# A planned feed-forward stage takes over the computed end times of the stage before it, and the last norm joins the plan

## The chip, the cores and the metric

The kernel runs on one core of one Trainium2 chip, in one launch. The metric is device time in microseconds from the first to the last instruction with what lies around it; lower is better. TensorE is called PE here, VectorE DVE, ScalarE ACT, GpSimd POOL; SP is the engine that issues most of the loads and stores.

## The reference

One layer of a hybrid decoder: two half-step SwiGLU feed-forward parts around a token mixer, and a norm over each row at the end. All values are fp32; 256 tokens, a width of 2048, a feed-forward width of 5632.

```python
def rms_norm(x, gain):
    var = mean(x * x, axis=-1); return x * rsqrt(var + 1e-6) * gain

def swiglu_ffn(x, w_gate, w_up, w_down):
    return (silu(x @ w_gate) * (x @ w_up)) @ w_down

x = x + 0.5 * swiglu_ffn(rms_norm(x, ffn1_norm), ffn1_w_gate, ffn1_w_up, ffn1_w_down)
x = x + mixer(rms_norm(x, mix_norm))          # gated recurrence and short convolution
x = x + 0.5 * swiglu_ffn(rms_norm(x, ffn2_norm), ffn2_w_gate, ffn2_w_up, ffn2_w_down)
return rms_norm(x, final_norm)
```

## The kernel before

**Tiling.** The 256 tokens are two row tiles, `t` = 0 and 1, of 128 each. `xres` holds the running sum; a chunk `c` is 512 of its 2048 columns. Hidden columns are treated in units of 512.

**Products.** An fp32 weight block is loaded into a `raw` tile and split into a high part (a rounding copy, `CAST` on ACT) and a low part (raw minus high, on DVE); PE multiplies high by the high and low parts of the other operand, and low by the high part. Blocks of two by two are multiplied with seven products instead of eight where sums allow it: a block ("sevens") has the units p0, p2, p3, p4, p5, p6, p1, whose weights or activations are sums of blocks, and x01, x00, x11, x10, which are plain. The weight sums are made by adding raw tiles, on DVE or by an accumulating DMA that POOL issues. Each unit adds into one of four PSUM banks, a, c, d and e; copies of a bank (`u_`, `s_`, or bank to bank) are taken on ACT between units. In a down stage `hv` is a sum of activations of two hidden units and `hs` its high and low part, the operand of p4, p5, p6 and p2.

**Stages.** Each feed-forward part (`tag` 1 and 2) begins with hand-ordered pieces (`first_blocks`, `fifth`, `down`). Then follow, for `s` = 1 and 3, a `fine_stage` (two gate blocks and two up blocks) and a `down_stage` (two blocks) that adds its result to `xres`. The results of an up block are multiplied with the gates (`gated_by`, the tile `z`), turned by PE (`ph`), and split into the high and low parts of the hidden activations `h`.

**What sets the order.** Each of these stages is laid out by a `Plan`. A step has an engine, an estimated length, the steps it needs, an earliest time `at`, and perhaps a `due` time. PE's order, unit by unit, is written in the tables `down_orders` and `fine_orders` ("j" or "-" ahead says whether bank c starts from bank e, "T" is where activations are turned, "n0" and "n1" are pieces of the next stage's norm). For the other engines the plan takes, among the steps that could start soonest, the one with the earliest latest time. The instructions are then issued in that order, and each engine works its own queue in order: an instruction that waits holds all behind it on its engine.

**From stage to stage.** A plan's clock is zero at the estimated end of PE's work in the plan before. `settled` hands over the times at which engines and buffers come free. Three kinds of steps belong to results of the stage before but are issued in the next one: the residual updates (`handed`), the last two gating products (`tails`), and the splits of the last turned activations (`later`). In the kernel before these enter with fixed times:

```python
for fn in handed:
    plan.add("DVE", add_ps, fn, at=0.1, due=12.0)
...
for key, high, low in later:
    turned[key] = turned_parts(plan, high, low, at=-2.0)
for (fn, cell), at in zip(tails, (-3.3, 0.1)):
    cell["step"] = plan.add("DVE", add_ps, fn, at=at, due=2.0)
```

**The end.** In the last down stage of the second part, `last` squares each finished chunk on ACT and multiplies it with the gain on DVE. The last chunk of row t=0 comes out of PE in two halves of 256 columns (`ps_d_last`). After the plan, `finish` issues by hand, in program order: `close` for row t=1 (square, root, the factor `fr` by one refined step, scaling of the row in four pieces and four stores), then for each half of row t=0 the update of `xres`, its square and its product `y`, and after the second half the factor, the scaling and the stores.

Of the kernel before, what the change touches and what calls it, by code (L numbers as in the profile page):

```python
# [176 lines left out]
def hybrid_block(ctx: ExitStack, tc: tile.TileContext, a: dict, out: bass.AP):  # L177
# [40 lines left out]
    def bank(name):  # L218
        return psum.tile([P, 512], F32, tag="ps", name=name)
# [522 lines left out]
    def ffn(tag, norm, after, opening=False):  # L742
        with tc.tile_pool(name=f"ffn{tag}", bufs=1, side="left", reuse_waits="tile") as fp:
# [298 lines left out]
            def down():  # L1042
# [60 lines left out]
                return updates  # L1103
# [169 lines left out]
            def turn_item(plan, u, t, h, *needs, later=None):  # L1273
# [20 lines left out]
                if later is not None:  # L1294
                    later.append(((u, t), high, low))
                    return None
                return turned_parts(plan, high, low, a)

            def sevens(plan, w, cs, name, sf, rows, xs, rooms, order, pairs, result, fills=None, down=False, joint=False, final=None):
# [107 lines left out]
                for key in order:  # L1407
# [24 lines left out]
                    if final is not None and key == units_only[-1]:  # L1432

                        def halves(u=u, q=q):
                            hi, lo = u.tiles["hi"], u.tiles["lo"]
                            for o in (slice(0, CW // 2), slice(CW // 2, CW)):
                                final.append(bank(f"ps_{name}_last")[:, : CW // 2])
                                parts = [(hi[:, j, o], lo[:, j, o]) for j in range(UK)]
                                multiply([(final[-1], sf[q], True, True)], parts)

                        u.low = plan.add("PE", 24 * 0.12, halves, *u.hi, *u.lo, *(fills or {}).get(q, []))
                        u.high.append(u.low)
                        continue
# [43 lines left out]
            def up_result(plan, sg, later):  # L1487
                def result(t, n, ps, done, keys, snaps, made):
# [28 lines left out]
            def pinned(plan):  # L1517
# [7 lines left out]
                    ["-", "p0", "p4", "x01", "p2", "p5", "x11", "p6", "p1", "p3", "x10", "x00"],  # L1525
                ),
                (
                    ["j", "p0", "p4", "T", "x01", "x11", "p5", "p1", "p6", "x00", "p2", "x10", "p3"],
                    ["-", "p0", "p4", "n1", "p2", "p1", "n0", "p5", "x11", "p6", "x00", "x10", "x01", "p3"],
# [3 lines left out]
                    ["-", "p0", "p4", "x01", "p2", "p5", "x11", "p6", "x00", "p3", "x10", "p1"],  # L1533
# [24 lines left out]
            def fine_stage(s, free, ready, handed):  # L1558
                plan = Plan(free, ready)
                for fn in handed:  # L1560
                    plan.add("DVE", add_ps, fn, at=0.1, due=12.0)
# [26 lines left out]
                return plan, tails, later  # L1588

            def down_stage(s, free, ready, tails, later, final=None):  # L1590
                plan = Plan(free, ready)
                turned, cells = {}, []
                for key, high, low in later:
                    turned[key] = turned_parts(plan, high, low, at=-2.0)
                for (fn, cell), at in zip(tails, (-3.3, 0.1)):
# [77 lines left out]
                return plan, handed  # L1673
# [13 lines left out]
            for s in (1, 3):  # L1687
# [435 lines left out]
    def last(plan, c, t, z):  # L2123
        if "fin" not in held:
            held["fin"] = bigs.tile([P, D], F32, tag="big", name="fin")
            nc.scalar.dma_start(held["fin"], a["final_norm"].partition_broadcast(P))
            held["roots"] = []
        fin = held["fin"]
        if c == NC_D - 1:
            return  # L2130
# [15 lines left out]
        def gain():  # L2146
            lastgain = fin[:, D - CW :]
            dve.tensor_scalar(lastgain, lastgain, -0.5, None, op0=ALU.mult)

        squared = plan.add("ACT", 0.65, square, z, due=10.0)  # L2150
        plan.add("DVE", 0.65, lambda: dve.scalar_tensor_tensor(xr, xr, -0.5, fin[:, cs], op0=ALU.mult, op1=ALU.mult), squared, due=25.0)
        held.setdefault(("squared", t), []).append(squared)
        if len(held["squared", t]) == NC_D - 1:
            pre = plan.add("DVE", 0.4, before, *held["squared", t], due=4.0)
            plan.add("ACT", 0.3, lambda: act.activation(single("root"), held[t], AF.Sqrt), pre, due=4.0)
            if t == 0:
                plan.add("DVE", 0.35, gain, pre, due=4.0)

    def finish(keep, halves):
        y = [keep(f"y_{t}") for t in range(NT)]  # L2160
        Engine.pinned = True
        close(1, y[1], 0, 1)
        w = CW // 2
        for h in range(2):
            xh = xres[:, 0, D - CW + h * w : D - CW + (h + 1) * w]
            dve.scalar_tensor_tensor(xh, halves[h], 0.5, xh, op0=ALU.mult, op1=ALU.add)
            close(0, y[0], h, 2)

    def close(t, y3, h, n):

        fin, w = held["fin"], CW // n

        def single(tag):
            return work.tile([P, 1], F32, tag=tag, name=f"{tag}_{t}_{h}")

        o = slice(D - CW + h * w, D - CW + (h + 1) * w)
        part = single("part")
        junk = work.tile([P, CW], F32, tag="junk", name=f"junk_f_{t}_{h}", bufs=1)
        act.activation(junk[:, :w], xres[:, t, o], AF.Square, accum_out=part)
        dve.tensor_tensor(y3[:, h * w : (h + 1) * w], xres[:, t, o], fin[:, o], op=ALU.mult)  # L2180
        if h < n - 1:
            held["part"] = part
            return
# [50 lines left out]
```

## Time and profile before

| what | value |
|---|---|
| time, median of 3 runs | 1715.39 us (1714.71 to 1715.41) |
| profiled run, its own time | 1715.2 us |
| span of that execution | 1713.4 us |
| granted clock of TensorE | 0.999 |
| TensorE busy | 1700.1 us, 99% |
| VectorE busy | 1547.2 us, 90% |
| ScalarE busy | 1110.6 us, 65% |
| GpSimd busy | 56.0 us, 3% |
| HBM read | 339.82 MB |

Times within the profile are from the start of the span. A busy time is that of one engine; a row of the timeline gives start, length, engine, operation, result and operands, and in square brackets how long the engine had been idle and what released it. In the program's names a number of the buffer is left out, so that `lo_d_p` is the low part of the weights of any p unit of a down block, and `raw_d_w` any raw tile of them.

### The profile page before, as it was taken

To read this page: it belongs to the slowest core of one execution; us is meant where nothing else is said; L and a number is where in the kernel's file an instruction comes from. 1 tells how busy PE (TensorE), PEld (TensorE's weight loads), DVE (VectorE), ACT (ScalarE), POOL (GpSimd) and SP (SyncE) were. 2 spreads that over 40 slices of the span, in tenths; PEclk is the share of its full clock that TensorE was granted. 3 is DMA by queue.
4 is the path that set the end of the run, shared out by engine and by line. 5 is a ranking of instruction groups with operands and counts; after the bars stand their busy time and mean duration, and the time that the engine had idled before them with its cause. 6 is when DMAs were issued, how large, how long until landed. Compare 5 with 4: busy or idle time off the path is not lost.

```text
span 1713.4 us, 20419 instructions
## 1 busy us (share of the span) xinstructions
PE 1700.1 (99%) x7889; PEld 1417.1 (83%) x7889; DVE 1547.2 (90%) x1346; ACT 1110.6 (65%) x1360; POOL 56.0 (3%) x90
## 2 busy tenths in 40 slices
PE   9999999999999999999999999999999999999997
PEld 8888888878888888888888888888888878888886
DVE  7989999999899999887897888899899998999997
ACT  7666566656666668666966666656666665667664
POOL 0010000000000000000000000000000000000000
PEclk9999999999999999999999999999999999999999
DMA  8766876768868868755556675665768778876884
GB/s 286 234 219 196 257 252 224 246 198 258 264 212 272 267 179 266 240 168 184 174 196 200 218 255 162 213 240 173 248 218 272 257 221 238 296 233 212 248 248 145
DMA packets 183313, 389.38 MB, mean 227 GB/s; under 512 B 7604, under 2 KB 10544, under 8 KB 177968
## 3 DMA queue, kind: packets, MB, share of 16 engines
q1 hardware_dynamic: 174656, 340.81, 56.8%
q0 software_dynamic: 8384, 46.21, 14.0%
q8 instruction: 61, 1.00, 0.2%
q10 hardware_dynamic: 176, 1.06, 0.2%
q14 instruction: 36, 0.29, 0.0%
HBM read 339.82 MB, written 2.10 MB: 200 GB/s over the span
## 4 chain that ended last, share of the span: by engine, by line
PE 95%; DVE 3%; ACT 1%; DMA 1%; issue 1%; DVEq 0%; ACTq 0%
PE ps_in L43 10%; PE ps_g_a L43 10%; PE ps_u_a L43 10%; PE ps_d_a L43 9%; PE ps_u_c L43 6%; PE ps_g_c L43 6%; PE ps_d_c L43 5%; PE ps_g_d L43 4%; PE ps_d_d L43 4%; PE ps_u_d L43 4%; PE ps_d_e L43 4%; PE ps_d L43 3%; PE ps_g_e L43 3%; PE ps_o L43 3%; PE ps_u_e L43 3%; PE ps_g L43 2%
## 5 line engine op out<-in xcount | busy, mean ns | idle before, releaser
L43 ACT CAST hi_g_p<-raw_g_w 128x1024 fp32r<-128x1024 f32 (+1 forms) x112 | 138.8, 1264 | 87.7 <-DVE raw_g_w L43 36.5
L43 ACT CAST hi_u_p<-raw_u_w 128x1024 fp32r<-128x1024 f32 x112 | 138.3, 1262 | 82.8 <-PE ps_u_a L43 27.3
L43 DVE TENSOR_TENSOR lo_u_p<-raw_u_w,hi_u_p 128x2560 fp32r<-128x2560 f32 (+2 forms) x72 | 160.1, 2229 | 15.1 <-ACT hi_u_p L43 12.6
L43 DVE TENSOR_TENSOR lo_g_p<-raw_g_w,hi_g_p 128x2560 fp32r<-128x2560 f32 (+2 forms) x72 | 160.3, 2229 | 14.2 <-ACT hi_g_p L43 7.7
L43 ACT CAST hi_d_p<-raw_d_w 128x1024 fp32r<-128x1024 f32 x112 | 112.5, 1046 | 61.0 <-DVE raw_d_w L43 33.8
L43 DVE TENSOR_TENSOR lo_d_p<-raw_d_w,hi_d_p 128x2048 fp32r<-128x2048 f32 (+1 forms) x72 | 129.8, 1813 | 4.7 <-ACT hi_d_p L43 4.6
L43 PE MATMUL ps_in<-xT_nm,hi_in 128*128 128x512 f32 x512 | 123.5, 392 | 0.0
L43 PEld LDWEIGHTS ps_in<-xT_nm,hi_in 128*128 128x128 f32 x512 | 94.0, 188 | 18.6 <-ACT tha L43 0.5
L43 DVE TENSOR_TENSOR lo_in<-raw_in,hi_in 128x2048 fp32r<-128x2048 f32 x32 | 73.3, 2290 | 21.3 <-ACT hi_in L43 19.3
L43 ACT CAST hi_in<-raw_in 128x1024 fp32r<-128x1024 f32 x64 | 64.1, 1044 | 30.5 <-PE ps_in L43 16.2
L43 ACT CAST hi_d_x<-raw_d_x 128x1024 fp32r<-128x1024 f32 x64 | 64.7, 1046 | 23.9 <-PE ps_u_d L43 10.1
L43 DVE TENSOR_TENSOR lo_d_x<-raw_d_x,hi_d_x 128x2048 fp32r<-128x2048 f32 x32 | 72.9, 2287 | 3.2 <-ACT hi_d_x L43 3.2
L43 DVE TENSOR_TENSOR raw_u_w<-raw_u_w,raw_u_w 128x1024 f32<-128x1024 f32 (+2 forms) x40 | 69.5, 1755 | 0.9 <-DMA raw_u_w<-in_ffn_w_up_dram 0.3
L43 DVE TENSOR_TENSOR raw_g_w<-raw_g_w,raw_g_w 128x1024 f32<-128x1024 f32 (+2 forms) x40 | 69.2, 1755 | 0.4
L43 PEld LDWEIGHTS ps_in<-xT_nm,lo_in 128*128 128x128 f32 x512 | 65.6, 191 | 2.5
L43 PE MATMUL ps_in<-xT_nm,lo_in 128*128 128x256 f32 x512 | 66.4, 283 | 0.0
L43 DVE TENSOR_TENSOR lo_g_x<-raw_g_x,hi_g_x 128x1536 fp32r<-128x1536 f32 x32 | 56.1, 1753 | 2.7 <-ACT hi_g_x L43 2.7
L43 PE MATMUL ps_u_a<-hi_u_p,x 128*128 128x512 f32 x224 | 56.8, 390 | 0.0
L43 PE MATMUL ps_g_a<-hi_g_p,x 128*128 128x512 f32 x224 | 56.6, 389 | 0.0
L43 ACT CAST hi_u_x<-raw_u_x 128x1536 fp32r<-128x1536 f32 x32 | 47.3, 1477 | 13.7 <-PE ps_u_c L43 5.7
L43 DVE TENSOR_TENSOR lo_u_x<-raw_u_x,hi_u_x 128x1536 fp32r<-128x1536 f32 x32 | 56.1, 1752 | 0.0
L43 ACT CAST hi_g_x<-raw_g_x 128x1536 fp32r<-128x1536 f32 x32 | 47.4, 1480 | 10.3 <-DMA raw_g_x<-in_ffn_w_gate_dram 6.5
(522 smaller groups left out, 4247.4 us busy)
## 6 DMA issues: line engine op xcount, KB each, us to landing
raw_g_w<-in_ffn_w_gate_dram SPq DMA_DIRECT2D x32, 1024.0 KB, 7.3
raw_u_w<-in_ffn_w_up_dram SPq DMA_DIRECT2D x32, 1024.0 KB, 6.4
raw_d_w<-in_ffn_w_down_dram SPq DMA_DIRECT2D x32, 1024.0 KB, 6.0
raw_d_x<-in_ffn_w_down_dram SPq DMA_DIRECT2D x32, 1024.0 KB, 6.1
raw_in<-in_w_in_dram SPq DMA_DIRECT2D x32, 1024.0 KB, 5.0
raw_d<-in_ffn_w_down_dram SPq DMA_DIRECT2D x24, 1024.0 KB, 5.2
raw_g_x<-in_ffn_w_gate_dram SPq DMA_DIRECT2D x32, 768.0 KB, 7.3
raw_u_x<-in_ffn_w_up_dram SPq DMA_DIRECT2D x32, 768.0 KB, 6.9
```

The source lines that it names most:

```text
L43: ins = getattr(self.engine, name)(*args, **kwargs)
```

## The change

The change does four things.

1. `fine_stage` and `down_stage` return, with each handed step, the time at which the plan that made it expects its operand, less that plan's end of PE; the next plan takes this as `at`.
2. Seven rows of the order tables are changed: three of the four blocks of the first fine stage, and four of the six rows for down stages. In one block bank c now starts from bank e ("j").
3. The last norm is laid out in the plan: `close_in` for row t=1, `close_half` for the two halves of row t=0, `row_out` for factor, scaling and stores. The gain step for the last chunk (`lastgain` times -0.5) is moved to the start of the last stage, and the gain of the third chunk of row t=0 behind the second half's update.
4. In the last norm, the product `y` of row t=0 is one instruction of 512 columns instead of two of 256, and of row t=1 ACT scales two pieces of 640 columns, where DVE scaled one of them.

```diff
-                return updates
+                return [(fn, 0.1) for fn in updates]
...
-                    later.append(((u, t), high, low))
+                    later.append(((u, t), high, low, a))
...
-                        later.append((gated_by, cell))
+                        later.append((gated_by, cell, done))
...
-                        later.append(lambda: update(c, t, ps()))
+                        later.append((lambda: update(c, t, ps()), done))
...
-                    ["-", "p0", "p4", "x01", "p2", "p5", "x11", "p6", "x00", "p3", "x10", "p1"],
+                    ["-", "p0", "p4", "x01", "p5", "x11", "p6", "x00", "x10", "p3", "p2", "p1"],
...
-                    ["-", "p0", "p4", "x01", "p5", "x11", "p2", "p6", "x00", "p3", "x10", "p1"],
+                    ["-", "p0", "p4", "x01", "p5", "p2", "x11", "p6", "x00", "p3", "x10", "p1"],
...
             def fine_stage(s, free, ready, handed):
                 plan = Plan(free, ready)
-                for fn in handed:
-                    plan.add("DVE", add_ps, fn, at=0.1, due=12.0)
+                for fn, at in handed:
+                    plan.add("DVE", add_ps, fn, at=at, due=12.0 - at)
...
-                return plan, tails, later
+                end = plan.free["PE"]
+                tails = [(fn, cell, max(done.end, cell["step"].end) - end) for fn, cell, done in tails]
+                return plan, tails, [(*z[:3], z[3].end - end) for z in later]
 
             def down_stage(s, free, ready, tails, later, final=None):
...
-                for key, high, low in later:
-                    turned[key] = turned_parts(plan, high, low, at=-2.0)
-                for (fn, cell), at in zip(tails, (-3.3, 0.1)):
+                for key, high, low, at in later:
+                    turned[key] = turned_parts(plan, high, low, at=at)
+                for fn, cell, at in tails:
                     cell["step"] = plan.add("DVE", add_ps, fn, at=at, due=2.0)
...
-                return plan, handed
+                end = plan.free["PE"]
+                return plan, [(fn, done.end - end) for fn, done in handed]
...
-                    final = [] if tag == 2 else None
-                    done, _ = down_stage(s + 1, free, ready, tails, later, final)
-                    if tag == 2:
-                        finish(keep, final)
+                    held["keep"] = keep
+                    done, _ = down_stage(s + 1, free, ready, tails, later, close_half if tag == 2 else None)
...
+    def row_out(plan, t, got, z, known, pieces):
...
+        b = plan.add("DVE", 0.65, gained, z, held["gain"], due=3.0)
+        c = plan.add("ACT", 0.3, root, *known, due=1.0)
+        d = plan.add("DVE", 0.75, factor, c, due=1.5)
+        before = {}
+        for engine, begin, end in pieces:
+            key = "ACT" if engine is act else "DVE"
+            before[key] = plan.add(
+                key, 0.1 + (end - begin) / 1000.0,
+                lambda z=(engine, begin, end): scaled_out(t, got["y"], got["r"], *z), d, b, *[before[k] for k in before if k == key],
+                *([got["third"]] if "third" in got and begin < 3 * CW < end + 1 else ()), due=5.0,
+            )
...
+    def close_half(plan, h, ps, done):
+        o = last_piece(h, 2)
+        xh = xres[:, 0, o]
...
+        z = plan.add(
+            "DVE", 0.43, lambda: dve.scalar_tensor_tensor(xh, ps(), 0.5, xh, op0=ALU.mult, op1=ALU.add), done,
+            *([ends["step"]] if h else ()), due=0.5,
+        )
+        a = plan.add("ACT", 0.6, square, z, *([ends["square"]] if h else ()), due=1.0)
+        ends["step"], ends["square"] = z, a
+        if not h:
+            ends["known"] = plan.add("DVE", 0.15, both, a, held["known", 0], due=1.0)
+            return
+        third, squared = ends["third"]
+        known = (a, ends["known"])
+        ends["third"] = plan.add("DVE", 0.65, third, squared, z, due=2.0)
+        pieces = (dve, 0, 256), (dve, 256, 896), (act, 896, 1536), (dve, 1536, 2048)
+        row_out(plan, 0, ends, z, known, pieces)
```

What this does to the queues is shown at three places. The first is VectorE at the entry to the first planned down stage of the first part (`d_2_0`): `z_2` are the two gating products that wait for the up block's last PSUM results, `hv_4_1` and `hs_2_4` the operand of p4, `h_6` a turned activation. Before:

```order
L43 TENSOR_TENSOR lo_d_2_0_p_2886<-raw_d_2_0_w_2871,hi_d_2_0_p_2879 128x2048
L43 TENSOR_TENSOR raw_d_2_0_w_2871<-raw_d_2_0_w_2873,raw_d_2_0_w_2871 128x1024
L43 TENSOR_TENSOR z_2_2568<-ps_u_2_a,z_2_2568 128x512
L43 TENSOR_TENSOR hv_4_1_2895<-h_4_2254 128x512
L43 TENSOR_TENSOR raw_d_2_0_w_2871<-raw_d_2_0_w_2873,raw_d_2_0_w_2871 128x1024
L43 TENSOR_TENSOR hv_4_1_2895<-hv_3_1_2882,hv_4_1_2895 128x512
L43 TENSOR_TENSOR lo_d_2_0_p_2904<-raw_d_2_0_w_2871,hi_d_2_0_p_2893 128x1024
L43 TENSOR_TENSOR z_2_2596<-ps_u_2_d,z_2_2596 128x512
L43 TENSOR_TENSOR hs_2_4_1_2918<-hv_4_1_2895,hs_2_4_0_2915 128x512
L43 TENSOR_TENSOR h_6_2898<-ph_6_1_2826,h_6_2898 128x4x128
L43 TENSOR_TENSOR h_6_2898<-ph_6_0_2831,h_6_2898 128x4x128
L43 TENSOR_TENSOR lo_d_2_0_p_2904<-raw_d_2_0_w_2871,hi_d_2_0_p_2893 128x1024
```

The same place of VectorE's queue in the changed kernel:

```order
L43 TENSOR_TENSOR lo_d_2_0_p_2886<-raw_d_2_0_w_2871,hi_d_2_0_p_2879 128x2048
L43 TENSOR_TENSOR raw_d_2_0_w_2871<-raw_d_2_0_w_2873,raw_d_2_0_w_2871 128x1024
L43 TENSOR_TENSOR hv_4_1_2892<-h_4_2237 128x512
L43 TENSOR_TENSOR raw_d_2_0_w_2871<-raw_d_2_0_w_2873,raw_d_2_0_w_2871 128x1024
L43 TENSOR_TENSOR hv_4_1_2892<-hv_3_1_2882,hv_4_1_2892 128x512
L43 TENSOR_TENSOR z_2_2568<-ps_u_2_a,z_2_2568 128x512
L43 TENSOR_TENSOR z_2_2596<-ps_u_2_d,z_2_2596 128x512
L43 TENSOR_TENSOR hs_2_4_1_2915<-hv_4_1_2892,hs_2_4_0_2901 128x512
L43 TENSOR_TENSOR lo_d_2_0_p_2918<-raw_d_2_0_w_2871,hi_d_2_0_p_2894 128x1024 x2
L43 TENSOR_TENSOR h_6_2913<-ph_6_1_2826,h_6_2913 128x4x128
L43 TENSOR_TENSOR h_6_2913<-ph_6_0_2831,h_6_2913 128x4x128
```

Both `z` moved behind the sum of `hv`, and the low half of `hs` now stands ahead of both pieces of p4's low weights. The second part has the same at its own first down stage.

The second place is SP's queue in the last down stage of the second part: `w` tiles are for p units, `x` tiles for x units, and the last three of each list are the ones whose order differs. Before:

```order
L43 DMA raw_d_4_1_w_13085<-in_ffn_w_down_dram 128x4x512
L43 DMA raw_d_4_1_x_13094<-in_ffn_w_down_dram 128x4x512
L43 DMA raw_d_4_1_w_13182<-in_ffn_w_down_dram 128x4x512
L43 DMA raw_d_4_1_x_13223<-in_ffn_w_down_dram 128x4x512
L43 DMA raw_d_4_1_x_13251<-in_ffn_w_down_dram 128x4x512
```

And SP's queue at that place now:

```order
L43 DMA raw_d_4_1_w_13083<-in_ffn_w_down_dram 128x4x512
L43 DMA raw_d_4_1_x_13092<-in_ffn_w_down_dram 128x4x512
L43 DMA raw_d_4_1_x_13181<-in_ffn_w_down_dram 128x4x512
L43 DMA raw_d_4_1_w_13243<-in_ffn_w_down_dram 128x4x512
L43 DMA raw_d_4_1_x_13255<-in_ffn_w_down_dram 128x4x512
```

The load of x00 moved ahead of p1's weights (13182, now 13243), which are the second addend for p3 too and stand now just ahead of x10's tile; POOL's last accumulating transfer waits for this addend in both kernels.

The third place is VectorE's queue at the end, from the update with the first half of the last PSUM result to the scaling. Before:

```order
L43 SCALAR_TENSOR_TENSOR xres<-ps_d_4_1_last,xres 128x256
L43 TENSOR_TENSOR y_13426<-xres,fin 128x256
L43 SCALAR_TENSOR_TENSOR xres<-ps_d_4_1_last,xres 128x256
L43 TENSOR_TENSOR y_13426<-xres,fin 128x256
L43 SCALAR_TENSOR_TENSOR pre_0_1_13459<-part_0_13450,pre_13315 128x1
L43 RECIPROCAL fy_1_13462<-fy_1_13462 128x1
L43 SCALAR_TENSOR_TENSOR fv_1_13461<-part_1_13455,pre_0_1_13459 128x1
L43 SCALAR_TENSOR_TENSOR fq_1_13463<-fv_1_13461,fy_1_13462 128x1
L43 SCALAR_TENSOR_TENSOR fr_1_13464<-fq_1_13463,fy_1_13462 128x1
```

VectorE's queue there in the changed kernel:

```order
L43 SCALAR_TENSOR_TENSOR xres<-ps_d_4_1_last,xres 128x256
L43 TENSOR_REDUCE pre_13441<-fss 128x1
L43 TENSOR_SCALAR pre_13441<-pre_13441 128x1
L43 SCALAR_TENSOR_TENSOR xres<-ps_d_4_1_last,xres 128x256
L43 SCALAR_TENSOR_TENSOR pre_0_0_13450<-part_0_13444,pre_13441 128x1
L43 SCALAR_TENSOR_TENSOR xres<-xres,fin 128x512
L43 TENSOR_TENSOR y_13458<-xres,fin 128x512
L43 SCALAR_TENSOR_TENSOR fv_0_13460<-part_1_13452,pre_0_0_13450 128x1
L43 RECIPROCAL fy_0_13456<-fy_0_13456 128x1
L43 SCALAR_TENSOR_TENSOR fq_0_13461<-fv_0_13460,fy_0_13456 128x1
L43 SCALAR_TENSOR_TENSOR fr_0_13462<-fq_0_13461,fy_0_13456 128x1
```

The product between the two halves is gone; a sum over the squares (`pre`), the gain of the third chunk (`xres<-xres,fin`) and one product of 512 columns now stand around the second half's update.

More of the change, by code (lines that the diff above doesn't have):

```diff
@@ L1524, in ffn @@
                     ["j", "p0", "p4", "T", "x01", "x11", "p5", "p1", "p6", "x00", "p3", "x10", "p2"],
[L1525 to L1529, printed above, removed]
+                    ["-", "p0", "p4", "x01", "p2", "p5", "x11", "p6", "p1", "p3", "x00", "x10"],
                 ),
@@ L2154, in last @@
             pre = plan.add("DVE", 0.4, before, *held["squared", t], due=4.0)
[L2155 to L2177, printed above, removed]
-        junk = work.tile([P, CW], F32, tag="junk", name=f"junk_f_{t}_{h}", bufs=1)
[L2179 to L2183, printed above, removed]
-        if n > 1:
-            pre = single("pre2")
-            dve.scalar_tensor_tensor(pre, held["part"], 1.0 / D, held[t], op0=ALU.mult, op1=ALU.add)
-            held[t] = pre
-        v, y, q, r = (single(f"f{k}") for k in "vyqr")
+            held["known", t] = plan.add("ACT", 0.3, lambda: act.activation(single("root"), held[t], AF.Sqrt), pre, due=4.0)
@@ new lines, in close_in, with square, both @@
+    def close_in(plan, t, z):
+        got = {}
+        def square():
+            got["part"] = square_last(t, 0, 1)
+        a = plan.add("ACT", 0.65, square, z, due=1.5)
+        pieces = (dve, 0, 256), (act, 256, 896), (act, 896, 1536), (dve, 1536, 2048)
+        row_out(plan, t, got, z, (a, held["known", t]), pieces)
+    ends = {}
+    def close_half(plan, h, ps, done):
+        o = last_piece(h, 2)
+        xh = xres[:, 0, o]
+        def square():
+            ends["part"] = square_last(0, h, 2)
+        def both():
+            pre = tiny("pre2", 0, 0)
+            dve.scalar_tensor_tensor(pre, ends["part"], 1.0 / D, held[0], op0=ALU.mult, op1=ALU.add)
+            held[0] = pre
+        z = plan.add(
[12 more added lines that the diff above has]
+        row_out(plan, 0, ends, z, known, pieces)
```

76 lines of the change are left out of this document (55 added, 21 removed), and 4 rows, old and new, of the table fine_orders.

## Prediction

> **What bounds the kernel now.** I read the page first, then the waits of TensorE, then the timeline round each wait, and last the timeline of the end.
>
> ```profile
> span 1713.4 us, 20419 instructions
> PE 1700.1 (99%) x7889; PEld 1417.1 (83%) x7889; DVE 1547.2 (90%) x1346; ACT 1110.6 (65%) x1360; POOL 56.0 (3%) x90
> PE 95%; DVE 3%; ACT 1%; DMA 1%; issue 1%; DVEq 0%; ACTq 0%
> PE ps_d_e L43 <- DVE hs L43: 1.7, 2, 0.8
> ```
>
> The first row gives the profiled execution's span, the second the busy times, the third the chain that ended last, the fourth the longest wait of TensorE. TensorE is the bound: the change leaves its matmuls as they are, so it can gain only where TensorE stands still and after its last matmul. The largest wait stands there twice, at the first planned down stage of each feed-forward part. The stretch in the first one, start and length in us:
>
> ```profile
> 359.88 2.29 DVE L43 TENSOR_TENSOR lo_d_p<-raw_d_w,hi_d_p 128x2048 fp32r<-128x2048 f32 x1 [0.16 <-ACT hi_d_p L43]
> 362.21 1.22 DVE L43 TENSOR_TENSOR raw_d_w<-raw_d_w,raw_d_w 128x1024 f32<-128x1024 f32 x1
> 365.58 0.85 PE L43 MATMUL ps_u_d<-lo_u_x,x 128*128 128x512 f32 x3
> 365.78 0.69 DVE L43 TENSOR_TENSOR z<-ps_u_a,z 128x512 f32<-128x512 f32 x1 [2.35 <-PE ps_u_a L43]
> 366.39 0.68 DVE L43 TENSOR_TENSOR hv<-h 128x512 f32<-128x512 f32 x1
> 366.99 1.22 DVE L43 TENSOR_TENSOR raw_d_w<-raw_d_w,raw_d_w 128x1024 f32<-128x1024 f32 x1
> 368.13 0.69 DVE L43 TENSOR_TENSOR hv<-hv,hv 128x512 f32<-128x512 f32 x1
> 368.24 1.05 ACT L43 CAST hi_d_p<-raw_d_w 128x1024 fp32r<-128x1024 f32 x1 [0.20 <-DVE raw_d_w L43]
> 368.73 1.22 DVE L43 TENSOR_TENSOR lo_d_p<-raw_d_w,hi_d_p 128x1024 fp32r<-128x1024 f32 x1
> 368.97 1.07 PE L43 MATMUL ps_d_a<-lo_d_p,h 128*128 128x512 f32 x4
> 369.20 0.61 ACT L43 CAST hs<-hv 128x512 fp32r<-128x512 f32 x1
> 369.86 0.68 DVE L43 TENSOR_TENSOR z<-ps_u_d,z 128x512 f32<-128x512 f32 x1
> 369.88 0.49 PE L43 MATMUL ps_d_e<-hi_d_p,hs 128*128 128x512 f32 x1
> 370.46 0.68 DVE L43 TENSOR_TENSOR hs<-hv,hs 128x512 fp32r<-128x512 f32 x1
> 371.20 1.90 PE L43 MATMUL ps_d_e<-hi_d_p,hs 128*128 128x512 f32 x7 [0.84 <-DVE hs L43]
> 372.26 1.22 DVE L43 TENSOR_TENSOR lo_d_p<-raw_d_w,hi_d_p 128x1024 fp32r<-128x1024 f32 x1
> 372.94 1.33 PE L43 MATMUL ps_d_e<-lo_d_p,hs 128*128 128x512 f32 x4
> 374.11 1.03 PE L43 MATMUL ph<-ident,z 128*128 128x128 f32 x8
> ```
>
> VectorE stands idle for 2.35 us before 365.78, because the gating product `z` that waits for TensorE's last sums stands ahead of `hv`, which waits for nothing. So everything behind it, down to the low half of `hs` at 370.46 to 371.14, is late, and the second matmul of unit p4 starts 371.20 - 369.88 = 1.32 us after the first. A matmul of this size takes 0.227 us start to start (four from 368.97 to 369.88). The twelve of p4 take 374.11 - 369.88 = 4.23 us and would take 12 x 0.227 = 2.72: 1.51 us are lost. The other feed-forward part:
>
> ```profile
> 1376.47 0.49 PE L43 MATMUL ps_d_e<-hi_d_p,hs 128*128 128x512 f32 x1
> 1377.80 1.90 PE L43 MATMUL ps_d_e<-hi_d_p,hs 128*128 128x512 f32 x7 [0.84 <-DVE hs L43]
> 1380.70 1.03 PE L43 MATMUL ph<-ident,z 128*128 128x128 f32 x8
> ```
>
> Again 1380.70 - 1376.47 = 4.23 us.
>
> **The change part by part.** *The hand-over.* In the new order VectorE goes from the first raw sum (ends 363.43) straight to `hv`, the second raw sum, the sum of `hv`, and only then to the two `z`. Start to start these take 0.60, 1.14 and 0.60 (366.39 to 366.99 to 368.13 to 368.73): `hv` 363.4, raw sum 364.0 to 365.2, sum to 365.9. The first `z` cannot start before 365.78 and hardly waits; the second is free at 365.58 + 0.85 = 366.43 and runs 366.45 to 367.1. ScalarE's last piece of p4 (1.05) follows the raw sum, 365.3 to 366.3, then the high half of `hs` (0.61) to 366.9; the low half on VectorE runs 367.1 to 367.8, where p4 wants it at 369.9. Two us of room. p4's low weights, 2 x 1.14 behind that, end at 370.1; they are wanted eight matmuls after 369.88, at 371.7. What is late next would be the weights of x01 (2.29 us), done near 373.5 by this count and wanted only sixteen matmuls into x01, which begins 0.8 after the transposes (374.11, less 1.5): at 377. So the whole 1.51 goes, twice: 3.0 us. Bounds: only the named wait, 2 x (1.32 - 0.23) = 2.2, if the pieces of 0.1 to 0.2 round it stay; 3.0 at most.
>
> *New orders of units.* They change no matmul, only which weights are wanted when. In the first gate block there is a small wait, for ScalarE's snapshot:
>
> ```profile
> 230.30 0.77 PEld L43 LDWEIGHTS ps_g_a<-hi_g_x,x 128*128 128x128 f32 x4 [0.47 <-ACT u_g L43]
> ```
>
> Putting p2 ahead of x11 moves this place away from the snapshot; worth between nothing and 0.3, I take 0.2. Against it stands a chain that gets tighter: in the second half of the first down stage the low half of `hs` for p2 now stands behind two weight splits of 2.29 each, which I count as 0 to 0.5 us for each feed-forward part; I take 0.1 each, since by my count about 1 us of room is left.
>
> *The last down stage of the second part.* p2 moves from the fourth place to behind p3, x10 ahead of both. So x10's weights are wanted earlier and its load is issued close behind that for p3's second addend, ahead of POOL's accumulate transfer for p3.
>
> ```profile
> 1679.35 2.29 DVE L43 TENSOR_TENSOR lo_d_p<-raw_d_w,hi_d_p 128x2048 fp32r<-128x2048 f32 x1
> 1701.24 1.11 PE L43 MATMUL ps_d_last<-hi_d_p,h 128*128 128x256 f32 x8
> 1687.94 0.59 ACT L43 ACTIVATE u_d<-ps_d_a 128x512 f32<-128x512 f32 x1
> 1688.55 1.28 ACT L43 ACT_TABLE_LOAD   x1
> 1689.85 0.20 ACT L43 ACTIVATE root<-pre 128x1 f32<-128x1 f32 x1
> raw_d_w<-in_ffn_w_down_dram SPq DMA_DIRECT2D x1, 1024.0 KB, 6.0
> raw_d_x<-in_ffn_w_down_dram SPq DMA_DIRECT2D x1, 1024.0 KB, 9.1
> raw_d_w<-in_ffn_w_down_dram SPq DMA_DIRECT2D x1, 1024.0 KB, 9.8
> raw_g_x<-in_ffn_w_gate_dram SPq DMA_DIRECT2D x1, 768.0 KB, 14.1
> ```
>
> The last four rows are single loads, issue to landing: a lone one of this stage, the one that ran beside POOL's transfer here, the slowest of this stage and the slowest of the run. The last unit keeps its place at 1701.24, so in this clock p2's twelve matmuls would start 2.72 earlier, at 1698.5, p3's at 1695.8, and x10's twenty-four at 1690.4. The buffer of x10 comes free when p6's low half is made, at 1679.35 + 2.29 less the 2.72 by which p6 moves up: 1678.9. I let it land 7 us later, at 1686, between 6.0 and 9.1, as it shares the way with one load first and POOL's transfer for its last part only. Then ScalarE: x10's high casts to 1688 (two of 1.05), a square to 1688.7, p1's casts to 1690.7, the table load and the root to 1692.2, p3's casts to 1694.2. VectorE makes p3's low half to 1696.5, wanted eight matmuls after 1695.8, at 1697.6: 1.1 us of room; then a residual update (0.7) and p2's low half to 1699.5, wanted at 1700.3: 0.8 of room. No stall, but each us of a landing later than about 1687 is a us of wait.
>
> The Trainium skill, page "ScalarE: Activation LUTs", section "What ACT_TABLE_LOAD costs", gives about 2.66 us to a switch of tables: 1.28 for the load and 1.38 for a drain. The trace has the 1.28, but the root starts 0.02 us behind the load and the snapshot ahead ends 0.02 before it: no drain. By the page's figure the chain would be 1.4 us longer, with some 0.6 us of wait, and the sum 0.6 smaller.
>
> *The end.*
>
> ```profile
> 1702.05 0.68 DVE L43 TENSOR_TENSOR y<-xres,fin 128x512 f32<-128x512 f32 x1
> 1703.63 0.64 PE L43 MATMUL ps_d_last<-lo_d_p,h 128*128 128x256 f32 x4
> 1705.27 0.42 DVE L43 SCALAR_TENSOR_TENSOR xres<-ps_d_last,xres 128x256 f32<-128x256 f32 x1
> 1706.32 0.29 ACT L43 ACTIVATE fy<-part,pre 128x1 f32<-128x1 f32 x1
> 1707.16 0.16 DVE L43 SCALAR_TENSOR_TENSOR fr<-fq,fy 128x1 f32<-128x1 f32 x1
> ```
>
> TensorE ends at 1703.63 + 0.64 = 1704.27; the factor `fr` is ready at 1707.32, 3.05 later; scaling and writing out fill the 6.1 to the span's end and stay as they are. The second half's update starts 1.0 us after TensorE's end, because the other token row's scaling stands ahead. In the new order it follows TensorE at once; but two operations that stood elsewhere (a gain of the third chunk and the 512-wide `y`, 0.60 start to start each) come between it and the factor. From TensorE's end: update to 0.5, `pre` near 0.6, gain from 0.7, `y` from 1.3, the four small steps (0.7, from the root's end at 1706.61 to 1707.32) from 1.9: `fr` at 2.5 to 2.6 against 3.05. I take 0.5. Bounds: 1.0, if nothing came between (1705.27 to 1707.32 is 2.05), and a loss of 0.4 if p2's low half is late, since the first row's whole norm stands behind it.
>
> **Sum.** 3.0 + 0.2 - 0.2 + 0.5 = 3.5 us. The profiled run took 1715.2 us, the median is 1715.39; the waits are those of the kernel and not of that run, so I take it from the median: 1711.9 us.
>
> **The rivals.** *The wait moves* (0.17): with VectorE at 90%, the work put off behind `hs` comes due in the same stage, at p4 of its second half. For it speaks the chain of two splits ahead of p2's `hs`; against it the room of about 1 us. At 0.8 us a part the gain is 1.9: 1713.5.
> *x10's load is late* (0.15): it lands after 9.1 us, at 1688, so that 0.9 us of wait comes before the end, and the first row's norm takes most of the 0.5 there: 3.5 - 1.3 = 2.2, 1713.2.
> *Slower than before* (0.06): the load meets POOL's accumulate transfer and the one ahead of it, and takes the 14.1 us that one load took: 1693.1, 6 us past the limit of about 1687, and the end loses 0.4: 1715.4 - 3.0 + 6.0 + 0.4 = 1718.8 or a little more. It decides from a landing of about 10.5 us. Against it: in this stage no load of the down weights took over 9.9. The Trainium skill, page "DMA: Bandwidth & Descriptors", section "Queues, rings and completion order", says that each DMA engine takes turns between the queues with work, a packet at a time; the 9.1 beside POOL's transfer against 6.0 alone agrees, and by that rule alone the load would take at most twice the lone 6.0.
> *The hand-over doesn't clear the wait* (0.07): another operand of p4, a raw buffer or ScalarE's turn, is late at the same point; then only the end gains: 1714.7.
>
> **How the numbers follow.** My forecast has 0.55, but lies at the edge of what a measurement of this kernel can tell from no change, 0.2% or 3.4 us (1712.0): its own range is 1711.1 to 1712.6, from a gain of 4.3 (the upper bounds: 3.0, 0.3, 1.0) to one of 2.8 (the new orders and the end give back 0.7). I give its lower side more, as the 3.0 rests on quoted rows: 0.49 beyond the edge, 0.06 this side. Same: 0.06 + 0.17 + 0.15 + 0.07 = 0.45. Slower: 0.06. The range runs from 1710.8, a little below the forecast's own low end for the spread of runs, to 1715.0, over the rivals that gain.
>
> **What would show it.** In the waits of TensorE `ps_d_e <- DVE hs` is gone; in the timeline the low half of `hs` ends before 368 and p4's twelve matmuls take 2.8 us; `fr` stands 2.5 to 2.6 after TensorE's end; the span is near 1710. A new wait at `ps_d_c`, `ps_d_a` or `ps_d_e` in the down stages, named for `lo_d_p`, `hs` or a load, or an `fr` at 3 us, would make it wrong.

## The result and the profile after

The changed kernel takes 1710.45 us (median of 10 runs, 1708.35 to 1712.25), the kernel before 1714.85 in the same series (1713.26 to 1715.84): a ratio of 0.9978, 95% interval 0.9970 to 0.9987, that is 3.8 us less (2.2 to 5.1); the two medians are 4.4 apart. A second series gave 0.9983 (0.9974 to 0.9992); one of its runs, of 4438 us and far off all others, is left out. The first line of the page of the changed kernel, and below it the complete list of the waits of TensorE's matmuls (total, times, longest):

```profile
span 1709.8 us, 20426 instructions
```

```profile
PE pt_nm L43 <- DVE xT_nm L43: 1.2, 1, 1.2
PE idle L43 <- DVE ones L43: 1.1, 1, 1.1
PE ps_g L43 <- ACT hi_g L43: 0.2, 1, 0.2
```

The wait for `hs` is gone; another, at `pt_nm`, stands first now. The entry to the first planned down stage, in the timeline of the changed kernel:

```profile
362.74 0.69 DVE L43 TENSOR_TENSOR hv<-h 128x512 f32<-128x512 f32 x1
...
364.47 0.69 DVE L43 TENSOR_TENSOR hv<-hv,hv 128x512 f32<-128x512 f32 x1
...
365.17 0.69 DVE L43 TENSOR_TENSOR z<-ps_u_a,z 128x512 f32<-128x512 f32 x1
...
366.46 0.68 DVE L43 TENSOR_TENSOR hs<-hv,hs 128x512 fp32r<-128x512 f32 x1
367.06 2.36 DVE L43 TENSOR_TENSOR lo_d_p<-raw_d_w,hi_d_p 128x1024 fp32r<-128x1024 f32 x2
...
369.27 2.03 PE L43 MATMUL ps_d_e<-hi_d_p,hs 128*128 128x512 f32 x8
...
372.07 1.03 PE L43 MATMUL ph<-ident,z 128*128 128x128 f32 x8
...
1375.10 2.03 PE L43 MATMUL ps_d_e<-hi_d_p,hs 128*128 128x512 f32 x8
...
1377.89 1.03 PE L43 MATMUL ph<-ident,z 128*128 128x128 f32 x8
```

VectorE no longer stands idle ahead of `z`, which comes behind the sum of `hv` now. The low half of `hs` ends at 367.14, 2.1 us before p4 wants it, and p4's twelve matmuls take 2.80 us (372.07 - 369.27) and 2.79, where both took 4.23: 1.43 and 1.44 gained. The end:

```profile
1700.82 0.64 PE L43 MATMUL ps_d_last<-lo_d_p,h 128*128 128x256 f32 x4
...
1701.50 0.42 DVE L43 SCALAR_TENSOR_TENSOR xres<-ps_d_last,xres 128x256 f32<-128x256 f32 x1 [0.74 <-PE ps_d_last L43]
...
1703.62 0.16 DVE L43 SCALAR_TENSOR_TENSOR fr<-fq,fy 128x1 f32<-128x1 f32 x1
...
1705.60 0.41 SPq L2199 DMA_DIRECT2D out_dram<-y  x1
```

TensorE ends at 1701.46 and `fr` is ready at 1703.78, 2.32 later (3.05 before); the last store is issued 4.14 after TensorE's end.

The new first wait is where the mixer begins. The rows are those of the changed kernel:

```profile
685.12 2.00 ACT L43 CAST hi_d_x<-raw_d_x 128x1024 fp32r<-128x1024 f32 x2 [1.36 <-DMA raw_d_x<-in_ffn_w_down_dram]
...
706.90 0.44 PE L43 MATMUL pt_nm<-ident,xres 128*128 128x128 f32 x2 [1.15 <-DVE xT_nm L43]
```

and this the second one's counterpart before:

```profile
708.14 0.44 PE L43 MATMUL pt_nm<-ident,xres 128*128 128x128 f32 x2 [0.27 <-DVE xT_nm L43]
```

TensorE's matmul waits 1.15 us there, where it waited 0.27: 0.9 us of the gain is given back. The experiments below were made to find what each part brings, and where this wait comes from.

### The profile page after: what moved, and what is told of

It is laid out like the page before. It is cut to its first block, busy times and chain, and to the rows that moved or that the text cites. A ratio compares the mean times of both kernels' runs of the same rounds, so it can differ in the third digit from the quotient of the medians.

```text
span 1709.8 us, 20426 instructions
## 1 busy us (share of the span) xinstructions
PE 1699.0 (99%) x7889; PEld 1417.8 (83%) x7889; DVE 1545.9 (90%) x1343; ACT 1110.4 (65%) x1361; POOL 56.0 (3%) x90
## 4 chain that ended last, share of the span: by engine, by line
PE 97%; DMA 1%; DVE 1%; ACT 1%; issue 0%; DVEq 0%; SPq 0%; ACTq 0%
PE ps_u_a L43 10%; PE ps_g_a L43 10%; PE ps_in L43 10%; PE ps_d_a L43 8%; PE ps_u_c L43 6%; PE ps_g_c L43 6%; PE ps_d_c L43 5%; PE ps_u_d L43 4%; PE ps_g_d L43 4%; PE ps_d_d L43 4%; PE ps_d L43 4%; PE ps_d_e L43 3%; PE ps_g_e L43 3%; PE ps_g L43 3%; PE ps_o L43 3%; PE ps_u L43 3%
```

## Experiments: the three parts by themselves

**The hand-over alone**, in the kernel before (tables and hand-issued end old).

```diff
-    for fn in handed: plan.add("DVE", add_ps, fn, at=0.1, due=12.0)
+    for fn, at in handed: plan.add("DVE", add_ps, fn, at=at, due=12.0 - at)
-    turned[key] = turned_parts(plan, high, low, at=-2.0)
+    turned[key] = turned_parts(plan, high, low, at=at)
-    for (fn, cell), at in zip(tails, (-3.3, 0.1)):
+    for fn, cell, at in tails:
```

> The kernel before with the hand-over times alone; order tables and the hand-issued end stay as before. Theory A (the hand-over clears the wait at p4 of the first planned down stage, and that is most of the gain): no wait ps_d_e <- DVE hs; TensorE ends 2.8 to 3.2 us earlier than the 1704.3 of before (1701.1 to 1701.5), span about 1710.4, some 3.0 us below before. Rival B (the new order tables are what gains; with the old tables the wait only moves): span 1712.5 or more, with a new wait in the down stages.

Measured: ratio 0.9988 (0.9979 to 0.9997), 2.1 us less (0.5 to 3.6). Besides `idle` at the start (1.1) and `ps_g` (0.2), which the changed kernel has too, TensorE's waits that are left are these:

```profile
PE pb_n L43 <- DVE diag_n L43: 0.6, 1, 0.6
PE pt_nm L43 <- DVE xT_nm L43: 0.4, 1, 0.4
```

The wait for `hs` is gone without any new order, and nothing new took its place in the down stages: p4's twelve matmuls take 2.80 us in both parts (370.60 - 367.80 and 1376.01 - 1373.21). Theory A stands. TensorE ends at 1699.58 in this profile, 4.7 us earlier than before, where 2.8 to 3.2 were expected. But 2.1 of the 4.7 are there before the first planned stage begins: TensorE's last stretch of `ps_d` ahead of it starts at 185.17, and at 187.25 in the kernel before. Over all profiles this stretch, ahead of which the change touches nothing, starts anywhere from 185.05 to 187.46, so spans and ends of single profiles are not compared in what follows.

**The tables alone** (the seven rows of the order tables, all else as before).

```diff
-    ["-", "p0", "p4", "x01", "p2", "p5", "x11", "p6", "x00", "p3", "x10", "p1"],
+    ["-", "p0", "p4", "x01", "p5", "x11", "p6", "x00", "x10", "p3", "p2", "p1"],
...
```

> The kernel before with the order tables alone; hand-over at the fixed times and the hand-issued end as before. Theory A: the wait ps_d_e <- DVE hs stays at about 1.7 us in two; the small wait at 230.3 goes (0.3); at the mixer's entry the wait of pt_nm grows from 0.3 to about 1.2, since the load for x01 of the first part's last stage now stands behind the mixer's first load; span 1713.5 to 1714.5, no gain. Rival B: span 1712 or less.

Measured: ratio 1.0017 (1.0008 to 1.0026), 2.9 us more. TensorE's two longest waits, and two rows of the end:

```profile
PE ps_d_e L43 <- DVE hs L43: 1.7, 2, 0.8
PE pt_nm L43 <- DVE xT_nm L43: 1.1, 1, 1.1
```

```profile
1702.26 0.64 PE L43 MATMUL ps_d_last<-lo_d_p,h 128*128 128x256 f32 x4
...
1707.91 0.16 DVE L43 SCALAR_TENSOR_TENSOR fr<-fq,fy 128x1 f32<-128x1 f32 x1
```

Rival B falls: the tables by themselves make the kernel slower. The wait at `pt_nm` comes with them, as theory A said, but the larger loss was in nobody's expectation: `fr` stands 5.17 us after TensorE's end (1708.07 - 1702.90), 2.1 later than before. With p2 now next to last, the third chunk of row t=0 is done late, and the hand-issued end begins only behind that chunk's square, root and gain (behind 1702.2) with the first row's norm, which the second row's then follows.

**The planned end alone** (hand-over and tables old). With the old order its row t=0 takes the norm before one share of the last chunk, that from bank d, is added; so that share is left out of the norm of this row.

```diff
-    finish(keep, final)
+    ... down_stage(s + 1, free, ready, tails, later, close_half if tag == 2 else None)
```

> The planned end alone: hand-over at the fixed times and the order tables of before. Theory A: TensorE ends as before (1704.3), the wait for hs stays, the factor of the last row is ready 2.3 to 2.7 us after TensorE's end instead of 3.05, span 0.4 to 0.8 us below before (1712.6 to 1713.0). Rival C (the end gained only because the new order of the last stage makes VectorE free in time): factor at 3 us, span as before.

Measured: ratio 1.0000 (0.9991 to 1.0009).

```profile
1703.54 0.64 PE L43 MATMUL ps_d_last<-lo_d_p,h 128*128 128x256 f32 x4
...
1706.32 0.16 DVE L43 SCALAR_TENSOR_TENSOR fr<-fq,fy 128x1 f32<-128x1 f32 x1
...
1709.01 0.40 SPq L2199 DMA_DIRECT2D out_dram<-y  x1
```

and the last store of the kernel before:

```profile
1709.13 0.41 SPq L2201 DMA_DIRECT2D out_dram<-y  x1
```

`fr` comes 2.30 us after TensorE's end, as theory A had it, but `y` and the late update of bank d now stand behind it, and the last store is issued 4.83 us after TensorE's end; before it was 1709.13 - 1704.27 = 4.86. So the time, and in substance the reason, are rival C's, though not the late factor that it expected: the end gained nothing by itself.

**Hand-over and tables, without the planned end.**

```diff
-    done, _ = down_stage(s + 1, free, ready, tails, later, close_half if tag == 2 else None)
+    done, _ = down_stage(s + 1, free, ready, tails, later, final)
+    if tag == 2: finish(keep, final)
```

> The changed kernel with the hand-issued end of before: hand-over times and all order tables new. Theory A (with the new order of the last stage the hand-issued end is late, as in the run of the tables alone; the planned end gains only together with it): the factor of the last row stands about 5.2 us after TensorE's end, 2.8 us later than in the changed kernel, and the time is 2 to 3.5 us above the changed kernel's, about that of before. Rival H (the late end belonged to the fixed hand-over times): the factor at about 3 us and the time within 1 us of the changed kernel.

Measured: ratio 1.0003 (0.9994 to 1.0012).

```profile
1700.78 0.64 PE L43 MATMUL ps_d_last<-lo_d_p,h 128*128 128x256 f32 x4
...
1706.43 0.16 DVE L43 SCALAR_TENSOR_TENSOR fr<-fq,fy 128x1 f32<-128x1 f32 x1
...
1708.40 0.41 SPq L2204 DMA_DIRECT2D out_dram<-y  x1
```

`fr` comes again 5.17 us after TensorE's end, the last store 6.98. Theory A stands, rival H falls. So tables and end belong together: from TensorE's end to the last store's issue it takes 4.86 with both old, 6.98 with the new tables alone, 4.83 with the planned end alone, and 4.14 with both. The 0.7 us of the end is what the pair gains; neither gains by itself.

## Experiments: where the hand-over's room and limits are

**Only the gating products at computed times** (and the residual updates): the kernel of the hand-over alone, with the splits of the last turned activations at -2.0 again.

```diff
-    return plan, tails, [(*z[:3], z[3].end - end) for z in later]
+    return plan, tails, [(*z[:3], -2.0) for z in later]
```

> The kernel before with computed times for the last two gating products (and the residual updates) alone; the splits of the last turned activations keep the fixed -2.0. Theory A (the products z ahead of hv are the whole cause of the wait): the p4 stretch loses 1.3 to 1.5 us in each part, as with the whole hand-over. Rival I (ScalarE's splits of h, which enter at -2.0, hold the high half of hs as well): a wait of 0.3 us or more for ACT hs or hi_d_p stays at p4.

Measured once (1712.2 us): the wait at p4 in the timeline, and what holds it.

```profile
365.56 1.08 ACT L43 CAST h<-ph 128x512 fp32r<-128x512 f32 x2 [1.63 <-PE ph L43]
...
366.52 0.63 ACT L43 CAST hs<-hv 128x512 fp32r<-128x512 f32 x1
367.04 1.06 ACT L43 CAST hi_d_p<-raw_d_w 128x1024 fp32r<-128x1024 f32 x1
...
368.49 2.03 PE L43 MATMUL ps_d_e<-hi_d_p,hs 128*128 128x512 f32 x8
368.93 1.28 DVE L43 TENSOR_TENSOR h<-ph,h 128x512 fp32r<-128x512 f32 x2
...
371.40 0.73 PE L43 MATMUL ps_d_e<-lo_d_p,hs 128*128 128x512 f32 x2 [0.42 <-DVE lo_d_p L43]
371.97 1.03 PE L43 MATMUL ph<-ident,z 128*128 128x128 f32 x8
```

The first of these rows has its counterpart in the kernel before, with the same idle time:

```profile
366.96 1.08 ACT L43 CAST h<-ph 128x512 fp32r<-128x512 f32 x2 [1.63 <-PE ph L43]
```

p4 takes 371.97 - 368.49 = 3.48 us: of the 1.43 about half is gained (0.75), and so it is in the second part. Theory A was too narrow. A split of `h` that waits for TensorE's turn stands ahead of the high half of `hs`, and ScalarE stands idle for 1.63 us for it. VectorE's share of the same splits (368.93) stands ahead of the last piece of p4's low weights, which begins only at 370.13, and for this piece TensorE waits 0.4 us in each part. So rival I has the cause right, ScalarE's early splits, though the wait is named for `lo_d_p`. With the times of the splits computed too the other 0.68 is gained: both kinds of handed steps had to move.

**VectorE's room.** The first sum of `hv` is made seven times.

```diff
-    e21, e22 = exact(1, p), exact(1, q)
+    e21, e22 = exact(1, p), exact(1, q, times=7 if s == 2 else 1)
```

> The changed kernel with the first sum of hv made seven times instead of once at the entry to the first planned down stage of each part: 3.6 us more of VectorE's time ahead of z and hs, the same order. Theory A (the chain hv, hs on VectorE has 2.1 us of room there, and it is what stood late before): the low half of hs ends near 370.7, TensorE waits at p4 again, ps_d_e <- DVE hs about 1.1 each, and p4's stretch grows by 1.3 to 1.8 us in each part, so that TensorE ends 2.6 to 3.6 us later than in the changed kernel. Rival F (VectorE's place doesn't matter, another operand cleared the wait): no wait for hs, under 1 us in all.

Measured once (1715.07 us): two of TensorE's waits, and rows of the timeline at the first part.

```profile
PE ps_d_e L43 <- ACT hs L43: 2.3, 2, 1.1
...
PE ps_d_e L43 <- DVE hs L43: 0.6, 2, 0.3
```

```profile
361.18 5.04 DVE L43 TENSOR_TENSOR hv<-h 128x512 f32<-128x512 f32 x7
...
366.80 1.07 PE L43 MATMUL ps_d_a<-lo_d_p,h 128*128 128x512 f32 x4
...
367.39 1.05 ACT L43 CAST hi_d_p<-raw_d_w 128x1024 fp32r<-128x1024 f32 x1 [4.24 <-DVE raw_d_w L43]
...
372.65 1.03 PE L43 MATMUL ph<-ident,z 128*128 128x128 f32 x8
```

and the row of the changed kernel from which its stretch is counted:

```profile
368.36 1.08 PE L43 MATMUL ps_d_a<-lo_d_p,h 128*128 128x512 f32 x4
```

The seven take 5.04 us instead of 0.69, 4.35 more (I had counted 3.6). From the start of the four matmuls ahead of p4 to the turn behind it TensorE takes 5.85 us, where the changed kernel takes 372.07 - 368.36 = 3.71: 2.14 more, where 1.3 to 1.8 were expected of the 3.6. So 4.35 - 2.14 = 2.2 us were absorbed: that is the room of VectorE's queue, against the 2.1 read off above. The wait is back, though named for ScalarE first, which stands idle for 4.24 us for the raw sum behind the seven and splits `hv` only after it. Theory A stands, rival F falls.

**A late x10**, the price of the rival that ended slower: its load is made twice, in a row, into the same tile.

```diff
+    for again in range(2 if name == "d2_4_1_x10" else 1):
```

> The changed kernel with the load of x10's weights in the last down stage of the second part made twice, one after the other, into the same tile, so that its use starts at the second landing. Theory A (1.0 us of room from the landing at 1682.6, then each us is a us of wait for TensorE at x10, p3 or p2): the second landing is at 1688 to 1690.5, TensorE's end moves by the landing less 1683.7, so 4 to 7 us, and the kernel is slower than before. Rival G (the chain behind the landing has slack that the count missed): under half of that.

Measured once: 1719.07 us. The timeline with the cast that waits for the second landing, and below it two stretches of TensorE (start and end, length, busy time with matmuls, granted clock, share and GB/s of the DMA):

```profile
1686.75 1.07 PE L43 MATMUL ps_d_a<-lo_d_x,h 128*128 128x512 f32 x4
1690.73 1.99 ACT L43 CAST hi_d_x<-raw_d_x 128x1024 fp32r<-128x1024 f32 x2 [7.72 <-DMA raw_d_x<-in_ffn_w_down_dram]
1691.83 3.78 PE L43 MATMUL ps_d_a<-hi_d_x,h 128*128 128x512 f32 x8 [4.01 <-ACT hi_d_x L43]
...
1705.71 1.11 PE L43 MATMUL ps_d_last<-hi_d_p,h 128*128 128x256 f32 x8
```

```profile
1691.80:1695.40 3.60, 3.57 (x8) 0.50 0.00 0
1695.40:1698.40 3.00, 3.00 (x9) 0.58 0.00 0
```

The second load takes 7.5 us from issue to landing and lands at 1690.6. In the changed kernel the one load took 6.4 us and landed at 1682.6, 8.0 earlier. From 1686.75 to the last unit TensorE takes 18.96 us; the changed kernel takes 1698.43 - 1686.64 = 11.79. So 7.2 us are lost, and the time is 8.0 above the changed kernel's of the same chip: about the price that was worked out, but not in the way it was worked out. TensorE waits 4.0 us for x10's first weights. Another 3.0 are lost behind the wait, where the profile shows no further one: x10's first sixteen matmuls take 6.59 us (1691.83 to 1698.42) against 3.63 in the changed kernel (1687.55 to 1691.18), at a granted clock of 0.50 and 0.58 against 1.00 there. The weights of p3 and p2, whose room was counted, come in time even so. So this run neither measures that room nor shows that each us late is a us of wait. Rival G's number (under half) did not come, but the slack that it names is there: on ScalarE the 0.57 us of idle time ahead of p1's casts, which the changed kernel has, are gone here, and the count had not seen them.

## Experiments: the wait at the mixer's entry

**The changed kernel with both order rows of the first part's last down stage put back.**

```diff
-    ["j", "p0", "p4", "T", "x01", "x11", "p5", "p1", "p6", "x00", "p3", "p2", "x10"],
-    ["j", "p0", "p4", "n1", "p1", "p2", "n0", "p5", "x11", "p6", "x00", "x10", "x01", "p3"],
+    ["j", "p0", "p4", "T", "x01", "x11", "p5", "p1", "p6", "x00", "p2", "x10", "p3"],
+    ["-", "p0", "p4", "n1", "p2", "p1", "n0", "p5", "x11", "p6", "x00", "x10", "x01", "p3"],
```

> The changed kernel with the two order rows of the first part's last down stage put back. Theory A (those rows put the mixer's first load ahead of the load for x01, so x01 and what follows on VectorE are late against TensorE): the wait of pt_nm for xT_nm falls from 1.2 to 0.3 or less, span 0.7 to 1.0 us below that of the changed kernel (about 1708.9). Rival D (the wait at the mixer's entry grew only because TensorE came there earlier, while loads and VectorE did not): it stays at 1.0 to 1.3, span as the changed kernel's 1709.8.

Measured: ratio 0.9975 (0.9966 to 0.9985), and the wait at `pt_nm` is 0.3 us.

**One mark put back**, with the changed kernel beside it on the same chip:

```diff
-    ["j", "p0", "p4", "n1", "p1", "p2", "n0", "p5", "x11", "p6", "x00", "x10", "x01", "p3"],
+    ["-", "p0", "p4", "n1", "p1", "p2", "n0", "p5", "x11", "p6", "x00", "x10", "x01", "p3"],
```

> The changed kernel itself once more, as the mate of the other kernels of this chip. Every theory: a ratio of 0.997 to 0.9987 to the kernel before; its profile shows the wait of pt_nm again at about 1.2 us, no wait for hs, and the factor of the last row 2.3 us after TensorE's end. What differs from the first profile of it is the spread of places that the change doesn't touch (the first 12 us, the hand-ordered down pieces near 145, the mixer's end near 1027).

> The changed kernel with one mark put back: in the second block of the first part's last down stage bank c is again kept apart from bank e ('-' for 'j'); all orders of units stay new. In the queue of SP the load for x01 then stands again ahead of the mixer's first load. Theory A (that place in SP's queue makes the mixer's entry late): the wait of pt_nm falls from about 1.2 to 0.5 or less, and the span by 0.6 to 1.2 us against the changed kernel. Rival D (TensorE simply comes there earlier than the loads and VectorE): the wait stays at 1.0 or more, time as the changed kernel's.

The changed kernel again: 1711.05 us, ratio 0.9983, the wait at `pt_nm` again 1.2. With the one mark: 1709.75 us, ratio 0.9976 (0.9967 to 0.9985). These are all waits of its matmuls:

```profile
PE idle L43 <- DVE ones L43: 1.1, 1, 1.1
PE ps_g L43 <- ACT hi_g L43: 0.2, 1, 0.2
```

SP's queue in the changed kernel at the load for x01 in the first part's last stage, and this load, issue to landing, in the changed kernel and with the mark put back:

```profile
675.55 0.37 SPq L43 DMA_DIRECT2D raw_in<-in_w_in_dram  x1
676.01 0.46 SPq L43 DMA_DIRECT2D raw_d_x<-in_ffn_w_down_dram  x1
```

```profile
raw_d_x<-in_ffn_w_down_dram SPq DMA_DIRECT2D x1, 1024.0 KB, 9.0
```

```profile
raw_d_x<-in_ffn_w_down_dram SPq DMA_DIRECT2D x1, 1024.0 KB, 6.8
```

Both are issued at about 676.0, each in the time of its own profile, but in the changed kernel the mixer's first load stands 0.5 us ahead of it on SP's queue. It lands at 685.0 instead of 682.8, ScalarE waits 1.36 us for it, the split of x01, VectorE's steps for the mixer's operands and the last residual updates follow late, and TensorE pays at `pt_nm`. With the mark back the wait is gone altogether. From its first `pt_nm` to its first `ps_o` TensorE takes 224.2 us before and with the hand-over alone, 225.1 in the changed kernel, 225.0 with the tables alone and 223.9 with the mark put back. So theory A holds, rival D falls: the loss comes with the tables, whether TensorE comes early or not. The mark does more than order the loads, as bank c starts from bank e with it; what ties the wait to the load is ScalarE's 1.36 us. Between these two kernels the means differ by 1.3 us with a standard error of 0.5 (10 and 11 runs). Of all versions run, the two changed kernels with the old load order there have the lowest ratios, though 0.9975 and 0.9976 can't be told from the 0.9978 of the changed kernel's first series.

## Why the prediction was right, and where not

- *What bounds the kernel.* Right: what was gained and lost are waits of TensorE and the stretch behind its last matmul.
- *The hand-over, 3.0 us.* Right in place and mechanism, 2.87 measured (1.43 and 1.44). Of each 4.23 a stretch of 2.80 is left against 2.72 by the nominal count. The working named VectorE's idle time as the cause, and let ScalarE's split of `hs` come in time without a word on what stood ahead of it. The early splits of `h`, for which ScalarE stood idle 1.63 us, were about as much of the loss (0.68 against 0.75), as the run with the gating products alone shows. The whole came out because the change moves both.
- *New orders, +0.2 and -0.2.* Here the step failed. The small wait at 230.3 is gone, 0.3 us (the twelve matmuls from 228.73 took 3.06 us, the same twelve take 2.72 now), and none of the chains that I feared in the second half of the first down stage waits. But the working followed SP's queue in the second part's last stage alone. In the first part's last stage the new row put the mixer's first load ahead of x01's, and cost 0.9 us at a place where no unit's order had changed. Every queue that a reordering passes had to be counted, in each stage whose rows changed.
- *The last down stage.* Right for the load as it came: a landing at 1682.6 (the count: 1686 on the old time axis, which runs 2.8 us later here, so 1683.2), and no wait. The 6.0 that it took for a lone load's time was not quite that: POOL's transfer, issued at 1663.40, took 7.3 us and ran beside its first 2.9 us; the load for p3's second addend in the changed kernel, without such company, took 5.1. The low halves for p3 and p2 end at 1693.70 and 1696.50 and are wanted at 1694.80 and 1697.52, 1.1 and 1.0 us of room where 1.1 and 0.8 were counted. The root starts 0.02 us behind the table load again (1687.99 + 1.28, 1689.29), so no drain is seen here either. The price of a later landing, a us for each us, is not shown: the load made twice lost 4.0 us to the wait and 3.0 to a lower granted clock.
- *The end, 0.5 us.* Right in sign, 0.73 at `fr`: `pre` was ready sooner than counted, and the gain behind it starts 0.44 us after TensorE's end and not 0.7. That the working treats it as a term by itself was wrong: it is what the new order and the planned end gain together, and with only one of them it would have been 0 or -2.1.
- *The sum.* The terms as measured are 2.87 + 0.3 - 0.9 + 0.7 = 3.0, inside the intervals of both series (2.2 to 5.1, and 1.4 to 4.5). By the first ratio the 1715.39 that the forecast started from becomes 1711.6, against the 1711.9 forecast; the 1710.45 is lower in part since the kernel before ran 0.5 faster in that series too. That 3.5 came so near is in part luck: the end, the small wait and the chains that cost nothing gave 0.5 more than counted, the hand-over 0.1 less, and 0.9 was missed.
- *The rivals.* "The wait moves" to p4 of the second half did not happen; a wait grew at the mixer's entry, which no rival named. "The hand-over doesn't clear the wait" did not happen with the whole change, but half of it did with the gating products alone, by way of ScalarE as it says; by its own terms its time is 1714.9 and not 1714.7, as 0.5 of 1715.39 is all that it leaves. "x10's load is late" and "slower than before" did not happen, and the load made twice shows a loss of the size that they reckon with, but another make-up of it.

## What to carry to other kernels

A step that waits for another engine, put at the head of an in-order queue by a constant that is too early, delays work that waits for nothing; look for it as idle time on an engine that is not the bound, just ahead of the bound's wait, and look on each engine, for one may hide the other. After any reordering, read the load queue of every stage whose rows changed: one load slipped ahead of another cost here a third of what the repair gained, and at a place 20 us further on. And try the parts of a change alone and together: of three parts here one gained by itself, one nothing, and one lost. When a long wait is made to price a late load, read the granted clock behind it: here 3.0 of 7.2 us were not wait.

## What was not expected of the hardware

After the wait of 4.0 us at x10, TensorE's granted clock in the profile was 0.50 for 3.6 us and 0.58 over the next 3.0, and then 1.00 again; behind the wait of 1.15 us at p4, with the sum made seven times, it stayed at 1.00 (366.8 to 373). An operation that reads the same operands and writes the same tile again and again takes 0.72 us from start to start (5.04 for seven), instead of the 0.60 in a row of different ones (1.28 for two); whether the reading or the writing costs the 0.12 is not shown. And places of the program that nothing here touched differ from profile to profile: the wait of `ps_d` for `h` near 146 stood at 0.4 us in the profile before and was absent after, that of `pb_n` for `diag_n` near 1027 ranged from absent to 1.0 us.
